# Hybrid attention block on one Trainium2 core: the last two of seven Strassen-like products change places

## The chip, the core and the metric

The kernel runs on one core of one Trainium2 chip as a single program that fills five engines: TensorE (PE, with its weight loads shown apart as PEld), VectorE (DVE), ScalarE (ACT), GpSimd (POOL) and SyncE (SP), of which SP does nothing here but issue DMAs. The metric is device time in microseconds (us) of one execution. The kernel before the change takes 705.33 us in the median of three runs (704.71 to 705.42).

## The reference

The reference computes one decoder block over 512 tokens, with 16 meta tokens put in front (528 positions), at a width of 1024:

```
h    = layer_norm(concat(meta, x))
proj = h @ w_in                      # queries, keys, values, gates of two branches, merge gates
y_d  = rms_norm(softmax(q k^T/8 + alibi) differences @ v)     # 8 heads, two maps each
y_s  = stick_breaking(sigmoid(q k^T/8)) @ v                   # 16 heads of 64
br_d = (y_d * silu(g_d)) @ w_br_diff ;  br_s = (y_s * silu(g_s)) @ w_br_sb
out  = layer_norm(alpha*h + (sigmoid(m_d+b)*br_d + sigmoid(m_s+b)*br_s) @ w_out)[16:]
```

All inputs are float32. The kernel keeps that precision on TensorE by splitting each operand into a high part in the reduced format float32r and a low rest, and adds three products: high by high, high by low, low by high.

## The kernel before, in words

**Units.** The attention is cut into 16 units: eight differential heads, d0 to d7, and eight pairs of stick-breaking heads, s0 to s7. While unit `u` scores, transposes and multiplies its values, the kernel already projects the keys and values of unit `u+1`, the queries of unit `u+2` and some gates. The attention work is a list of steps with due times, the projections are Python generators that yield after each small group of matmuls, and `run` (L574) weaves the two: each yield adds to a clock (0.36 for each row block of the seven products, that is three matmuls), and all steps whose due time has come are emitted there. That gives the program order.

**Who sets the order on the engines.** Between L970 and the late stages the program order is only a priority. A planner, with a cost model of its own, walks through the instructions and gives each engine a fixed order: it puts the next ready instruction by priority, so that work that is later in the program can stand ahead of work that is waiting. On the chip each engine then runs its order as it stands and waits at semaphores. From a point in the last unit (`state["ends"]`, L1039) TensorE's order is the program's, and in the late stages that of all engines is.

**Keys and values by seven products.** For units 4 to 15 (d4 to d7 and s0 to s7) `stage_kv` (L681) makes the 256 columns of keys and values, over 528 positions, with seven block products in place of eight. Each product is 12 matmuls of 128x264 (four row blocks by three parts of the split). They accumulate in three PSUM banks:

- bank x takes products 0, 2, 4 and 6, one on top of the other. Between them x is read: into `u` after 0 (ACT, L711), into the values' buffer `vT` after 2 (ACT, L715), subtracted from `z7` into the second half of `vT` after 4 (DVE, L720), and read as the second half of the keys after 6;
- bank z takes product 1, read into `z7` (ACT, L713), and later product 5, which finishes the first half of `vT` (DVE, L722);
- bank y takes product 3, which with `u` makes the first half of the keys (DVE, L717).

A matmul that adds to a bank has to wait until the reader before it is done. `keys` (L704) splits a finished half of the keys into high and low (ACT L706, DVE L707) in a buffer `ks` (two of them), and `store_k` (L649) sends both halves with eight DMAs on SP's queue (L653, L654) into the tiles `K[0]` and `K[1]`. There is one such pair of tiles for all units, so the stores of unit `u+1` must stand behind the scores of unit `u` in the program.

**Weights.** The seven left factors are four blocks of the weights and sums of them. Two sums come from DMAs that add onto a loaded tile (issued by POOL, L147), and one, which the product into x that comes last needs, is added on DVE (`add`, L170) out of two others. `prep` (L194 to L204 with `hi` at L185 and `lo` at L190) runs four products ahead: it casts a factor to its high part (ACT, L185), takes the rest (DVE, L190), adds the sum if the next factor is one, and fetches further weight tiles (SP, L145) into rings of six and five buffers, as far as those have been used up. The list `items` says which loaded tiles make up each factor, in the order of the products.

**Scores of a stick-breaking pair.** `s_scores` (L900) does one head in five steps, from the longest block of keys down: two matmuls per block (L764), two sigmoids on ACT (L910, L912), a scan and a product on DVE (L916, L917). In unit s0 the sigmoids and the last normalisation of the branch before (L889 to L893, which needs another table of ACT's functions) are chained on ACT in program order (`behind`, L216).

Of the kernel before, what the change touches and what calls it, by code (L numbers as in the profile page):

```python
# [46 lines left out]
def hybrid_block_kernel(ctx: ExitStack, tc: tile.TileContext, x, meta, emb_g, emb_b, w_in, b_gate,  # L47
# [42 lines left out]
    items, names, loads = [], [], []  # L90
    for n, (kind, i) in enumerate(seq):
        if kind in ("BD", "BS", "wd", "ws"):
            if kind[0] == "B":
                tiles = [(w_br_d if kind == "BD" else w_br_s)[:, :, ts(2 * i + m, P)] for m in range(2)]
            else:
                tiles = [w_in[:, :, ds(COL[x + kind[1]] + i * P, P)] for x in "kv"]
            (a11, a12), (a21, a22) = [[w[:, ts(k, 4)] for k in range(2)] for w in tiles]
            ring = "rawa" if kind[0] == "B" else "rawk"
            o = len(loads)
            if ring == "rawa":  # L100
                loads += [(a11, None, "raw"), (a21, (a11,), ring), (a21, (a22,), ring), (a12, None, "raw"), (a22, None, "raw")]
                items += [o, o + 1, (o + 2, o), o + 3, o + 2, o + 4, (None, o + 3)]
            else:
                loads += [(a11, None, "raw"), (a21, (a11,), ring), (a21, (a22, a11), ring), (a12, None, "raw"),
                          (a21, (a22,), ring), (a22, None, "raw")]
                items += [o, o + 1, o + 2, o + 3, o + 4, o + 5, (o + 2, o + 3)]
        elif n < 4:
            items += [None, None]
        else:
            c = COL[kind] + i * P  # L110
            items += [len(loads), len(loads) + 1]
            loads += [(w_in[:, ts(k, 4), c:c + P], None, "raw") for k in range(2)]
        names += [(kind, i)] * (len(items) - len(names))
# [472 lines left out]
    with tc.tile_pool(name="att", bufs=1) as ap:  # L586
# [62 lines left out]
        def store_k():  # L649

            for o, t in staged:
                for c, own, _ in HEADS:
                    nc.sync.dma_start(K[c][LO, :, o].bitcast(F32), t[own].bitcast(F32))  # L653
                    nc.sync.dma_start(K[c][HI, 0, o].bitcast(F32), t[own, 0].bitcast(F32))  # L654
            staged.clear()
# [25 lines left out]
        def stage_kv(unit, kind, n):  # L681

            i = take("w" + kind, n, 7)
            x, z, y = [pj.tile([P, 512], F32, tag="pj", name="q")[:, :H2] for m in range(3)]
            if not kvt:
                kvt.append(pair_of("kvt"))
            u, z7 = kvt[0][:, 0, :H2], kvt[0][:, 0, H2:]

            vT = kvt[0][:, 1, :] if (UNITS.index((kind, n)) - SEVEN) % 2 == 0 else ap.tile([P, L], F32, tag="vT", name="vT")
            of = [(hTh, [hTl[:, k] for k in range(KT)], m, n) for m, n in ((0, 0), (4, 0), (4, 1))]  # L690
            of += [(tS[0], [tL[k % 4][:, k // 4] for k in range(KT)], m, n) for m, n in ((0, 1), (0, 0), (4, 1), (4, 0))]

            def product(q, bank, b, start=True):
                prep(i + q + state["ahead"])
                _, wh, wl = split[i + q]
                bh, bl, m, half = of[b]
                for k in range(4):
                    h, l = bh[:, m + k, ts(half, H2)], bl[m + k][:, ts(half, H2)]
                    for j, (a, b) in enumerate(((wh, h), (wh, l), (wl, h))):
                        pe.matmul(bank, a[:, k, :], b, start=start and k == 0 and j == 0,  # L700
                                  stop=k == 3 and j == 2, skip_group_check=not start)
                    yield 0.36

            def keys(m, src):  # L704
                t = ap.tile([P, 2, H2], F32R, tag="ks", name="ks", bufs=2)
                s.copy(t[:, 0], src)  # L706
                v.tensor_tensor(t[:, 1], src, t[:, 0].bitcast(F32), op=ALU.subtract)  # L707
                staged.append((ts(m, H2), t))

            yield from product(0, x, 0)  # L710
            s.copy(u, x)  # L711
            yield from product(1, z, 5)
            s.copy(z7, z)  # L713
            yield from product(2, x, 4, False)
            s.copy(vT[:, :H2], x)  # L715
            yield from product(3, y, 1)
            v.tensor_tensor(u, y, u, op=ALU.add)  # L717
            keys(0, u)
            yield from product(4, x, 3, False)
            v.tensor_tensor(vT[:, H2:], z7, x, op=ALU.subtract)  # L720
            yield from product(5, z, 6, False)
            v.tensor_tensor(vT[:, :H2], z, vT[:, :H2], op=ALU.subtract)  # L722
            unit["vT"] = vT
            yield from product(6, x, 2, False)
            keys(1, x)
            store_k()

        def values(unit, kind):

# [228 lines left out]
        def spread(gen, t0, dt, count):  # L958
            return [(t0 + dt * m, lambda: next(gen)) for m in range(count)]
# [12 lines left out]
        for u, (kind, n) in enumerate(UNITS):  # L972
            unit = units[u]
# [6 lines left out]
            steps = pending + [(0.6, lambda unit=unit: values(unit, kind))]  # L980
# [9 lines left out]
            if kind == "d":  # L990
                ta = {}
                dt, t0, t1 = TD[u in GATE_AT]
                steps += spread(d_scores(unit, n), 0.0, dt, 10)
                parts = transposed(ta, apads[n % 2])
                steps += [(t0 + 0.7 * m, f) for m, f in enumerate(parts)]
                steps.append((t1, lambda: d_values(unit, ta)))
                pending = [(3.0 if n < 7 else 5.8, lambda unit=unit, n=n: d_norm(unit, n))]
            else:
                if n == 0:
                    diag.append(ap.tile([P, L], F32, tag="bias", name="diag", bufs=2))  # L1000
                    g.memset(diag[0], 0.0)
                    g.tensor_copy(diag[0][:, L - P:], ident)
                    g.memset(v3[:, 1], 0.0)
                    for a in apads:
                        for i in range(NB):
                            g.memset(a[:, ds(AOFF[i] + NKEY[i] - 1, 1)], 0.0)
                if last:
                    ydT = [pair_of("ydT", n=S) for k in range(4)]
                    ydT = [ydT[k % 4][:, k // 4, :] for k in range(8)]
                    ysT = ypool.tile([P, 8, S], F32, tag="ys", name="ysT")  # L1010
                    ysT = [ysT[:, k, :] for k in range(8)]
                    unit["y"] = ysT[7]

                    def fill_in(y, of):
                        placed(lambda: nc.sync.dma_start(y, of), [mybir.EngineType.SP])

                    fill_in(ydT[7], kept["d"][7])
                    for m, (y, of) in enumerate(((ydT, "gd"), (ysT, "gs"))):
                        for j in range(7):
                            steps.append((1.3 + 1.5 * (7 * m + j), lambda o=y[j], x=kept[of][j]: fill_in(o, x)))  # L1020
                    proj += [gate("d", n, lambda: ydT[7]), merge_gate(0, 0), behind_values(merge_gate(0, 1)), merge_gate(0, 2),
                             gate("s", n, lambda: ysT[7])]
                else:
                    if GATE_AT.get(u) == n:
                        yd = gpool.tile([P, S], F32, tag="sg", name="yd")
                        nc.sync.dma_start(yd, kept["d"][n])
                        proj.append(gate("d", n, lambda yd=yd: yd, kept["gd"][n]))
                    else:
                        steps += zip((12.0, 24.0), late_gate(ap, *(kept[x][n] for x in ("d", "r", "gd"))))
                    proj.append(gate("s", n, lambda unit=unit: unit["y"], kept["gs"][n]))  # L1030
                for c in range(2):
                    ta = {}
                    steps += spread(s_scores(unit, c, n == 0), (2.0 + 4.3 * c) if n == 0 else 4.4 * c, 0.85, 5)
                    parts = transposed(ta, apads[c])
                    times = LAST[c] if last else [7.0 + 6.5 * c + 0.7 * m for m in range(3)] + [10.5 + 6.5 * c]
                    steps += zip(times, parts)
                    steps.append((times[3], lambda c=c, ta=ta: s_values(unit, c, n, ta)))
                if last:
                    steps.append((LAST[0][0] - 0.1, lambda: state.update(ends=len(nc.cur_bb.bb.instructions))))  # L1039
# [118 lines left out]
    for p in range(4):  # L1158
        steps = []
# [132 lines left out]
```

## Time and profile before

| | |
|---|---|
| median of three runs | 705.33 us (704.71 to 705.42) |
| the profiled execution | 705.11 us |
| span of its instructions | 703.3 us |
| PE busy | 695.7 us (99%) |
| DVE busy | 570.2 us (81%) |
| ACT busy | 441.5 us (63%) |
| POOL busy | 131.1 us (19%) |
| granted TensorE clock, mean | 0.999 |

The profile comes from one execution. Busy time is the time in which at least one instruction of an engine was running. The profile models when a matmul ends, and matmuls overlap in the pipeline: a 128x264 matmul has a duration of some 0.28 us, while the next one starts 0.12 us after it. So what TensorE really does is read from starts, and from the idle time and the waits that the profile lists. L12 means line 12 of the kernel.

### The profile page before, as it was taken

Reading aid. Unit: us, or ns where it says so; the run is one execution under the profiler, and the core shown is the slowest. Engines: PE = TensorE matmul, PEld = TensorE weight load, DVE = VectorE, ACT = ScalarE, POOL = GpSimd, SP = SyncE. Lnnn points to the kernel's source line nnn. Section 1 sums busy time; section 2 is a strip of 40 time slices with the busy share of each in tenths; the row PEclk is TensorE's granted clock in tenths of the full one; section 3 lists DMA queues with packets and bytes.
Section 4 is the critical chain, followed back from the end, with each engine's and each line's share of the span. In section 5 each row is a group of like instructions: output and inputs, shape, how many; then the busy total and the mean of one; then the engine's idle time right before and its main releaser. Section 6 shows DMA issues by size and latency. Waiting matters only on the chain.

```text
span 703.3 us, 13295 instructions
## 1 busy us (share of the span) xinstructions
PE 695.7 (99%) x4482; PEld 634.8 (90%) x4482; DVE 570.2 (81%) x1226; ACT 441.5 (63%) x1074; POOL 131.1 (19%) x141
## 2 busy tenths in 40 slices
PE   8999999999999999999999999999999999999997
PEld 8999999989899898999989899988888998999885
DVE  6887998978786777989887898977665888688887
ACT  5776767757576687777757687766555456555400
POOL 2243112222222201212121220000011201230012
PEclk9999999999999999999999999999999999999999
DMA  9399547978888786899798977547476749796702
GB/s 290 102 189 188 147 113 177 213 174 188 219 189 184 191 190 181 177 221 207 204 195 216 206 151 198 159 128 240 134 167 132 160 119 232 154 178 184 254 34 120
DMA packets 184214, 124.93 MB, mean 178 GB/s; under 512 B 8993, under 2 KB 168130, under 8 KB 184146
## 3 DMA queue, kind: packets, MB, share of 16 engines
q1 hardware_dynamic: 148050, 102.84, 50.5%
q0 software_dynamic: 35776, 20.19, 23.0%
q10 hardware_dynamic: 320, 1.06, 0.4%
q8 instruction: 35, 0.57, 0.3%
q14 instruction: 33, 0.27, 0.1%
HBM read 93.54 MB, written 9.44 MB: 146 GB/s over the span
## 4 chain that ended last, share of the span: by engine, by line
PE 93%; DVE 2%; ACT 2%; SPq 1%; DMA 1%; issue 0%; POOL 0%; POOLq 0%; ACTq 0%; DVEq 0%
PE q L700 18%; PE ps L500 12%; PE ps L499 12%; PE ps L501 12%; PE q L1083 11%; PE ps L515 6%; PE sc L764 6%; PE pso L1215 5%; PE t L776 4%; PE tv L733 1%; PE av L931 1%; PE av L932 1%; DMA xt<-in_x_dram 1%; PE av L925 1%; PE av L933 1%; PE av L926 1%
## 5 line engine op out<-in xcount | busy, mean ns | idle before, releaser
L500 PE MATMUL ps<-hTl,w 128*128 128x512 f32 x368 | 144.8, 393 | 0.0
L190 DVE TENSOR_TENSOR w<-raw,w 128x512 fp32r<-128x512 f32 x168 | 114.3, 688 | 37.5 <-ACT w L185 35.9
L499 PE MATMUL ps<-hTh,w 128*128 128x512 f32 x368 | 144.6, 393 | 0.0
L501 PE MATMUL ps<-hTh,w 128*128 128x512 f32 x368 | 144.6, 393 | 0.0
L185 ACT CAST w<-raw 128x512 fp32r<-128x512 f32 x168 | 103.4, 627 | 11.6 <-PE ps L501 5.4
L147 POOL DMA_DIRECT2D rawk<-in_w_in_dram x48 | 66.1, 1629 | 116.6 <-DMA rawk<-in_w_in_dram 58.2
L700 PE MATMUL q<-tS,w 128*128 128x264 f32 x384 | 82.6, 289 | 0.0
L1083 PE MATMUL q<-gh,w 128*128 128x256 f32 x448 | 81.4, 283 | 0.2 <-ACT t L1092 0.2
L501 PEld LDWEIGHTS ps<-hTh,w 128*128 128x128 f32 x368 | 69.2, 188 | 13.5
L499 PEld LDWEIGHTS ps<-hTh,w 128*128 128x128 f32 x368 | 69.2, 188 | 13.1
L500 PEld LDWEIGHTS ps<-hTl,w 128*128 128x128 f32 x368 | 69.2, 188 | 13.0
L1083 PEld LDWEIGHTS q<-gh,w 128*128 128x128 f32 x448 | 70.1, 192 | 0.5 <-ACT t L1092 0.4
L764 PE MATMUL sc<-k,A 128*128 128x264 f32 (+3 forms) x320 | 66.0, 299 | 0.0
L700 PEld LDWEIGHTS q<-tS,w 128*128 128x128 f32 x384 | 63.6, 188 | 0.3
L1083 PE MATMUL q<-gl,w 128*128 128x256 f32 x224 | 63.4, 283 | 0.0
L700 PE MATMUL q<-hTh,w 128*128 128x264 f32 x288 | 60.8, 286 | 0.0
L916 DVE TENSOR_TENSOR_SCAN e<-e,diag 128x528 f32<-128x528 f32 (+1 forms) x64 | 54.2, 850 | 5.7 <-ACT e L910 5.7
L700 PE MATMUL q<-tl,w 128*128 128x264 f32 x192 | 54.9, 286 | 0.0
L764 PEld LDWEIGHTS sc<-k,A 128*128 128x128 f32 x320 | 50.1, 189 | 2.3 <-POOL k L607 0.2
L515 PE MATMUL ps<-hTh,w 128*128 128x264 f32 x256 | 51.5, 289 | 0.2 <-ACT k L642 0.2
L700 PEld LDWEIGHTS q<-hTh,w 128*128 128x128 f32 x288 | 47.8, 189 | 1.0 <-DVE vT L720 0.2
L781 ACT CAST ah<-t 128x384 fp32r<-128x384 f32 (+2 forms) x72 | 34.4, 477 | 22.0 <-PE t L776 21.9
(292 smaller groups left out, 1575.9 us busy)
## 6 DMA issues: line engine op xcount, KB each, us to landing
raw<-in_w_in_dram SPq DMA_DIRECT2D x142, 256.0 KB, 3.4
rawk<-in_w_in_dram POOLq DMA_DIRECT2D x48, 256.0 KB, 5.8
rawk<-in_w_in_dram SPq DMA_DIRECT2D x36, 256.0 KB, 4.1
k<-ks SPq DMA_DIRECT2D x60, 132.0 KB, 3.0
raw<-in_w_out_dram SPq DMA_DIRECT2D x16, 256.0 KB, 4.1
k<-ks SPq DMA_DIRECT2D x60, 66.0 KB, 2.8
A<-low SPq DMA_DIRECT2D x28, 128.0 KB, 2.8
raw<-in_w_br_diff_dram SPq DMA_DIRECT2D x12, 256.0 KB, 2.9
```

The lines of the kernel that those rows point to most:

```text
L147: second[l] = [lambda raw=raw, x=x: g.dma_start(raw, x, accum_op=ALU.add) for x in more]
L185: s.copy(wh, raw)
L190: eng.tensor_tensor(wl, raw, wh.bitcast(F32), op=ALU.subtract)
L499: pe.matmul(ps, wh[:, k % 4, :], hTh[:, k, M:], start=(k == 0), stop=False)
L500: pe.matmul(ps, wh[:, k % 4, :], hTl[:, k, M:], start=False, stop=False)
L501: pe.matmul(ps, wl[:, k % 4, :], hTh[:, k, M:], start=False, stop=(k == KT - 1))
L515: pe.matmul(ps[:, :H2], a[:, k % 4, :], b[:, k, ts(c, H2)], start=(k == 0 and m == 0), stop=(k == KT - 1 and m == 2))
L700: pe.matmul(bank, a[:, k, :], b, start=start and k == 0 and j == 0, stop=k == 3 and j == 2, skip_group_check=not start)
L764: pe.matmul(ps[:, :n], q, K[:, m, k0:k0 + n], start=(m == 0), stop=(m == 1))
L916: v.tensor_tensor_scan(rev, rev, diag[0][:, L - nk:][:, ::-1], 0.0, ALU.mult, ALU.max)
L1083: pe.matmul(bank, a[:, k, :], b[:, n, k, :], start=start and k == 0 and m == 0, stop=k == 3 and m == 2, skip_group_check=not start)
L1215: pe.matmul(ps, MH[k][:, ts(t, P)] if m == "h" else ML[:, k, ts(t, P)], WO[c]["hl".index(w)][:, k, r], start=(n == 0), stop=(n == 3 * KT - 1))
```

## The change

The last two of the seven products change places: what was product 6 (into x, finishing the second half of the keys) becomes product 5, and what was product 5 (into z, finishing the first half of the values) becomes product 6. The list of factors changes places with them, so the factor that is a sum is now prepared as the sixth and the plain block as the seventh. The split of the second half of the keys and the eight stores stand ahead of the last product now. As the stores stand 12 matmuls earlier in the program, the second head of unit s0 gets earlier due times (5.2 to 8.6 in place of 6.3 to 9.7), so that its scores still stand ahead of the stores. No instruction is added or removed.

```diff
             else:
                 loads += [(a11, None, "raw"), (a21, (a11,), ring), (a21, (a22, a11), ring), (a12, None, "raw"),
                           (a21, (a22,), ring), (a22, None, "raw")]
-                items += [o, o + 1, o + 2, o + 3, o + 4, o + 5, (o + 2, o + 3)]
+                items += [o, o + 1, o + 2, o + 3, o + 4, (o + 2, o + 3), o + 5]
...
             yield from product(4, x, 3, False)
             v.tensor_tensor(vT[:, H2:], z7, x, op=ALU.subtract)
-            yield from product(5, z, 6, False)
+            yield from product(5, x, 2, False)
+            keys(1, x)
+            store_k()
+            yield from product(6, z, 6, False)
             v.tensor_tensor(vT[:, :H2], z, vT[:, :H2], op=ALU.subtract)
             unit["vT"] = vT
-            yield from product(6, x, 2, False)
-            keys(1, x)
-            store_k()
...
-                    steps += spread(s_scores(unit, c, n == 0), (2.0 + 4.3 * c) if n == 0 else 4.4 * c, 0.85, 5)
+                    steps += spread(s_scores(unit, c, n == 0), (2.0 + 3.2 * c) if n == 0 else 4.4 * c, 0.85, 5)
```

## The prediction

> **What bounds the kernel now.** I read the page first, then the busy time by stretches, then TensorE's waits, and last two of the twelve units in order of time. The page's first part and the stretches (per engine: busy us and number of instructions; the second stretch runs from the first of the seven products to the end of the last):
>
> ```profile
> PE 695.7 (99%) x4482; PEld 634.8 (90%) x4482; DVE 570.2 (81%) x1226; ACT 441.5 (63%) x1074; POOL 131.1 (19%) x141
> ```
>
> ```profile
> 0.00:107.40 107.40, 104.58 (x749) 99.38 (x750) 88.87 (x246) 71.25 (x185) 28.14 (x44) 1.00 0.71 171
> 107.40:452.00 344.60, 344.60 (x2275) 317.27 (x2275) 287.72 (x640) 249.54 (x647) 69.50 (x66) 1.00 0.84 192
> 452.00:650.00 198.00, 197.81 (x1222) 178.04 (x1221) 148.88 (x279) 111.15 (x227) 27.65 (x24) 1.00 0.69 168
> 650.00:703.30 53.30, 48.71 (x242) 40.14 (x240) 44.76 (x63) 9.55 (x17) 5.84 (x7) 0.98 0.37 137
> ```
>
> TensorE is busy for 344.60 of the 344.60 us in which the change acts, at full granted clock (1.00), and for 197.81 of the 198.00 us behind it. Its 7.6 us of idle time lie in the head (2.82) and the tail (4.59), which the change doesn't touch. The waits of matmuls, all five rows, and the one wait of a weight load on a reader of the seven products (total us, times, longest):
>
> ```profile
> PE warm L309 <- POOL ident masks.py:199: 1.4, 1, 1.4
> PE bank L344 <- DVE xn L340: 1.1, 1, 1.1
> PE centred L1237 <- ACT turned L1236: 0.9, 1, 0.9
> PE ps L515 <- ACT k L642: 0.2, 1, 0.2
> PE q L1083 <- ACT t L1092: 0.2, 1, 0.2
> ```
>
> ```profile
> PEld q L700 <- DVE vT L720: 0.2, 1, 0.2
> ```
>
> No row says that a matmul of the seven products, or a score, waits for keys. In twelve units the reader of x cost one weight load 0.2 us, once.
>
> Busy time can hide a short wait, since a 128x264 matmul is shown for 0.28 us and the next starts 0.12 us later. So I look at starts, in the last of the twelve (keys of s7). TensorE, then DVE:
>
> ```profile
> 444.32 0.28 PE L700 MATMUL q<-tl,w 128*128 128x264 f32 x1
> 444.44 0.29 PE L700 MATMUL q<-tS,w 128*128 128x264 f32 x1
> 444.57 0.40 PE L499 MATMUL ps<-hTh,w 128*128 128x512 f32 x1
> ...
> 449.38 0.39 PE L500 MATMUL ps<-hTl,w 128*128 128x512 f32 x1
> 449.61 0.39 PE L501 MATMUL ps<-hTh,w 128*128 128x512 f32 x1
> 449.84 0.29 PE L700 MATMUL q<-hTh,w 128*128 128x264 f32 x1
> ```
>
> ```profile
> 444.42 0.43 DVE L722 TENSOR_TENSOR vT<-q,vT 128x264 f32<-128x264 f32 x1
> ...
> 445.58 0.42 DVE L720 TENSOR_TENSOR vT<-kvt,q 128x264 f32<-128x264 f32 x1
> ```
>
> L722 reads z and L720 reads x after product 4, and L722 comes first: the planner had already put the z product ahead of product 4, though it stands behind it in the program. After x's product 4 ends (last start 444.44), TensorE takes a gate and attention work, and the last x product (on hTh) starts at 449.84, 3.84 us after L720 ended at 446.00. It follows its neighbour at 0.23 us, the step between two 128x512 matmuls (449.38 to 449.61): no wait is hidden there. A tighter hand-over, in the unit at 187 to 215 us (TensorE, then DVE):
>
> ```profile
> 199.06 0.41 PE L700 MATMUL q<-tS,w 128*128 128x264 f32 x2
> 199.31 0.59 PE L764 MATMUL sc<-k,A 128*128 128x272 f32 x4
> 199.73 0.44 PE L885 MATMUL ms<-sqh,onesm 128*128 128x512 f32 x1
> 200.01 0.40 PE L886 MATMUL ms<-sql,onesm 128*128 128x512 f32 x1
> 200.24 0.30 PE L700 MATMUL q<-hTh,w 128*128 128x264 f32 x1
> ```
>
> ```profile
> 199.67 0.42 DVE L720 TENSOR_TENSOR vT<-kvt,q 128x264 f32<-128x264 f32 x1
> ...
> 200.09 0.41 DVE L722 TENSOR_TENSOR vT<-q,vT 128x264 f32<-128x264 f32 x1
> ```
>
> L720 ends at 200.09, the x product starts at 200.24, again 0.23 us behind its neighbour. The planner filled the gap exactly.
>
> [...]
>
> **The change part by part.**
>
> *The matmuls.* 12 units by 84 matmuls, before as after, into the same banks: 0. On TensorE only what is exposed between them can change.
>
> *The new neighbour.* In the program the two x products now stand next to each other, with only L720 between them. From the start of product 4's last matmul to the end of L720 it took 446.00 - 444.44 = 1.56 us in the one unit and 200.09 - 199.06 = 1.03 us in the other; less the usual step of 0.12 us that is 0.9 to 1.4 us which something must cover. The cover is the z product, 12 by 0.12 = 1.4 us, which has been ready since z was copied early on, or the gates and scores that cover it in the rows above. If no cover were left it would be 12 x 0.9 to 12 x 1.4 = 11 to 17 us; at the size of the one wait listed, 12 x 0.2 = 2.4 us. From below: a hidden wait in the old hand-over is at most 0.28 - 0.12 = 0.16 us, 12 x 0.16 = 1.9 us that could be won. I take 0, since both hand-overs shown have nothing hidden and the chain of dependences in x and in z is the same as before; only priorities change.
>
> [...]
>
> *The factors.* Casts, rests and the DVE sum are as many as before; the sum moves one product forward, the plain block one back, and its ring buffer comes free one product later (1.4 us of matmuls), the buffer of the other summand one sooner. What the users of the factors waited for within the stretch (first rest for cast, then cast for TensorE):
>
> ```profile
>   ACT w L185: 16.9, 16
>   PE ps L501: 12.5, 16
>   PE q L700: 4.0, 8
> ```
>
> The casts wait for TensorE to give a buffer back, never for a weight load, so loads land before they are wanted and I take 0. The bound above: eight stores now stand ahead of the last product's load on SP. Here are the second half's first and last issues, the split ahead of them (ACT, DVE), the first score that uses them and the values' transposes:
>
> ```profile
> 452.94 0.52 SPq L654 DMA_DIRECT2D k<-ks  x1
> ...
> 456.76 0.60 SPq L654 DMA_DIRECT2D k<-ks  x1
> ```
>
> ```profile
> 452.23 0.38 ACT L706 CAST ks<-q 128x264 fp32r<-128x264 f32 x1
> ```
>
> ```profile
> 454.19 0.42 DVE L707 TENSOR_TENSOR ks<-q,ks 128x264 fp32r<-128x264 f32 x1
> ```
>
> ```profile
> 461.88 0.65 PE L764 MATMUL sc<-k,A 128*128 128x264 f32 x4
> ...
> 475.72 0.60 PE L733 MATMUL tv<-ident,vT 128*128 128x128 f32 x4
> ```
>
> Eight issues at 0.52 to 0.60 us are 4 to 5 us in which a weight load could stand in line, per unit; bounds 0 and 12 x 5 = 60 us if nothing were prepared ahead.
>
> *Keys sooner, values later.* The split costs 0.38 + 0.42 us, off TensorE, as before. What the swap can win for the keys is at most the 3.84 us by which the x product trailed L720. That would pull the first scores of s7 ahead from 461.88, but TensorE has no gap to fill until then: worth 0. The values get ready one product later, some 1.4 us; their transposes start at 475.72, 30.9 us after L722 ended at 444.85: 0. With the cover gone it would be those 1.4 us once per unit, 17 us.
>
> *Unit s0.* ACT's rows: the table load in front of the last normalisation, and the second head's first sigmoid after it; TensorE's row: the second head's first scores.
>
> ```profile
> 255.12 1.28 ACT L889 ACT_TABLE_LOAD   x1
> ...
> 265.08 0.39 ACT L910 ACTIVATE e<-sc 128x264 f32<-128x264 f32 x1
> ```
>
> ```profile
> 254.44 0.41 PE L764 MATMUL sc<-k,A 128*128 128x264 f32 x2
> ```
>
> The first pair of sigmoids (2 x 0.39 us) now comes ahead of that table load; the rest of the second head stays behind it, and the loads stay as many. A score's bank comes free some 10 us sooner; TensorE has no idle time here either, so 0, with at most 0.8 us of ACT as a loss.
>
> *Sum.* 703.3 us span + 0 + 0 + 0 + 0, and 1.8 us around it: 705.1 us against the profiled 705.11. That execution lies 0.2 us under the median and within the runs' spread; I predict **705.2 us**.
>
> **The rivals.**
>
> *It doesn't do what it says.* The planner goes by readiness: z's product was ahead of x's product 4 already, so the order on TensorE may hardly change and the keys end when they did. For it: L722 ahead of L720 in the one unit. Against it: in the other L722 came after. Time: 705.2 too.
>
> *Faster.* The hand-overs of x hide 0.16 us each after all, and the new order gives it back: 705.2 - 1.9 = 703.3 us. Against it: nothing hidden in either unit shown. More than that TensorE can't give.
>
> *Slower: x behind x.* Place: the first matmul of the new product 5, waiting for L720 with nothing between. It decides once the planner has used up z's product before product 4, as it did for s7, and finds no gate or score ready. Price: 705.2 + 2.4 = 707.6 us at the one wait listed, 716 to 722 us uncovered. For it: L722's early place. Against it: gates and scores filled the same gap in both units.
>
> *Slower: weights late.* SP's queue gets the stores first and a cast waits for its load. One wait as long as an issue, 0.6 us, in each unit: 705.2 + 7 = 712 us. Against it: casts never waited for a load.
>
> **How the numbers follow.** The forecast has 0.52, no change of order 0.23, faster 0.09, x behind x 0.12, late weights 0.04. A measurement tells about 0.2%, 1.4 us, from no change: the first two cases lie within it, so same 0.75, faster 0.09, slower 0.16. The range reaches from 704.2, the forecast less half of the 1.9 us, to 707.6, the cheap form of x behind x; that leaves out some 0.17.
>
> **What would show it right or wrong.** Right: TensorE without idle time up to the tail, L720 with other matmuls between it and x's next product, K's last issue before 456.76. Wrong: a wait of L700 on L720 in many units, casts that wait for a DMA of raw weights, idle TensorE between 107 and 452 us, or a tail that isn't 4.6 us.

## The result and the profile after

The changed kernel takes 710.97 us in the median (709.05 to 711.48), the kernel before on the same chip 705.38 us (704.66 to 705.57). The ratio is 1.0075, with an interval of 1.0064 to 1.0086: the change costs 5.6 us. The profiled execution took 711.42 us with a span of 709.6 us, so 6.3 us are to be found in the traces (709.6 - 703.3).

The page's first part, and the stretches with the bounds used before, without the head; the last one ends with the span:

```profile
PE 699.7 (99%) x4482; PEld 637.1 (90%) x4482; DVE 571.8 (81%) x1226; ACT 441.1 (62%) x1074; POOL 130.1 (18%) x141
```

```profile
107.40:452.00 344.60, 341.94 (x2240) 314.00 (x2239) 284.57 (x632) 244.57 (x635) 67.97 (x65) 1.00 0.84 189
...
650.00:709.60 59.60, 54.82 (x291) 46.07 (x289) 50.49 (x73) 14.27 (x28) 5.83 (x7) 1.00 0.41 143
```

The work is the same (4482 matmuls), but TensorE is now idle for 2.66 us in the stretch of the seven products, where it had no idle time, and gets 2240 matmuls done there in place of 2275. Its waits (total us, times, longest) name the places; rows that stood in the list before are left out:

```profile
PE sc L764 <- DMA k<-ks: 1.8, 1, 1.8
...
PE sc L764 <- ACT e L910: 0.8, 1, 0.8
PE av L925 <- ACT ys L942: 0.4, 1, 0.4
PE ps L499 <- DVE sg L529: 0.3, 1, 0.3
...
PE t L776 <- DVE al L782: 0.2, 1, 0.2
```

No matmul of the seven products waits, and none waits for L720. What waits are scores, twice, and three matmuls of the last unit. First the largest wait, on TensorE at the start of unit s3:

```profile
337.96 0.60 PE L776 MATMUL t<-ident,apad 128*128 128x128 f32 x4
340.37 0.48 PE L764 MATMUL sc<-k,A 128*128 128x264 f32 x2 [1.81 <-DMA k<-ks]
...
341.58 0.42 PE L700 MATMUL q<-tl,w 128*128 128x264 f32 x1
341.80 0.65 PE L700 MATMUL q<-tS,w 128*128 128x264 f32 x2
```

The scores on the second half of the keys come 1.98 us after their turn, worked out from the starts as everywhere below (340.37, less the start of the last transpose in front at 338.28, less its usual step of 0.11). Behind the gap a second loss follows: from 341.58 to 341.80 a step of 128x264 takes 0.22 us and not 0.12. Thirteen steps in a row are stretched like that, 1.37 us in all. The stretches show why (the granted clock is the third number from the right):

```profile
340.30:341.20 0.90, 0.83 (x7) 0.86 (x8) 0.00 (x0) 0.32 (x2) 0.00 (x0) 0.99 1.17 318
341.20:344.30 3.10, 3.10 (x17) 3.10 (x15) 2.57 (x3) 1.41 (x5) 0.00 (x0) 0.50 0.44 112
```

The trace has the clock at 0.50 from 341.18 to 344.59: TensorE runs for 3.4 us at half clock. PE counts as busy all the while (3.10 of 3.10 us in the second row), so the busy share doesn't show it.

The second wait of scores is that at the start of unit s5, 1.01 us at 406.1; the list names ACT L910 for it, but by the trace that was long done, and the store of K landed at 407.12, 0.14 us ahead of the score. The third place is the last unit. TensorE there, after and, for comparison, before:

```profile
474.19 0.71 PE L764 MATMUL sc<-k,A 128*128 128x144 f32 x4
475.27 0.49 PE L925 MATMUL av<-ah,V 128*128 128x512 f32 x1 [0.38 <-ACT ys L942]
475.92 0.55 PE L776 MATMUL t<-ident,apad 128*128 128x128 f32 x3 [0.15 <-DVE al L782]
476.72 0.50 PE L499 MATMUL ps<-hTh,w 128*128 128x512 f32 x1 [0.25 <-DVE sg L529]
```

```profile
467.08 0.86 PE L764 MATMUL sc<-k,A 128*128 128x400 f32 x4
467.78 0.39 PE L501 MATMUL ps<-hTh,w 128*128 128x512 f32 x1
...
469.16 0.40 PE L501 MATMUL ps<-hTh,w 128*128 128x512 f32 x1
469.40 0.49 PE L776 MATMUL t<-ident,apad 128*128 128x128 f32 x3
469.64 0.48 PE L925 MATMUL av<-ah,V 128*128 128x512 f32 x1
```

Before, seven gate matmuls (467.78 to 469.16) lay between the scores and the next product with the values; ACT copied the bank out in their shadow (L942, 467.53 to 468.11). After, they have been used up earlier, and the product follows the scores and waits for ACT: 0.54, 0.42 and 0.41 us, 1.37 in all.

The sum: 1.98 + 1.37 + 1.01 + 1.37 = 5.7 us of the 6.3. The rest is in steps that are each under 0.2 us too long.

**Why the keys of s3 are late.** They are finished later than before, not sooner. The rows of their last steps, before: DVE (the reader of x), TensorE (the last product into x, first and last rows), ACT and DVE (the split), SP (the store that the scores wait for, its landing, and the queries' DMAs), and the scores.

```profile
320.50 0.43 DVE L720 TENSOR_TENSOR vT<-kvt,q 128x264 f32<-128x264 f32 x1
...
328.93 0.41 DVE L707 TENSOR_TENSOR ks<-q,ks 128x264 fp32r<-128x264 f32 x1
```

```profile
324.54 0.29 PE L700 MATMUL q<-hTh,w 128*128 128x264 f32 x1
...
337.42 0.65 PE L764 MATMUL sc<-k,A 128*128 128x264 f32 x4
```

```profile
330.04 0.88 SPq L653 DMA_DIRECT2D k<-ks  x1
...
335.25 3.21 SPq L624 DMA_DIRECT2D A<-low  x2
```

```profile
DMA to landing us min/median/max: 4.6/4.6/4.6
```

And after:

```profile
323.73 0.42 DVE L720 TENSOR_TENSOR vT<-kvt,q 128x264 f32<-128x264 f32 x1
...
334.12 0.43 DVE L707 TENSOR_TENSOR ks<-q,ks 128x264 fp32r<-128x264 f32 x1
```

```profile
328.72 0.37 PE L700 MATMUL q<-hTh,w 128*128 128x264 f32 x1
```

```profile
335.06 1.37 SPq L624 DMA_DIRECT2D A<-low  x2
336.53 1.28 SPq L653 DMA_DIRECT2D k<-ks  x2
```

The rows of SP don't show which of the two heads a store is for; the built program does. The first scores of s3 are the first head's, and they need the second half of `K[0]`: before, that store is the one at 330.04 (the stores after it, up to 333.32, fill `K[1]` for the second head), and after, it is the first of the two at 336.53.

L720 ends 3.2 us later than before (324.15 for 320.93), the last product into x starts 4.2 us later, behind gate and query matmuls, the split on DVE is 5.2 us later, and on SP the store now stands behind two of the queries' DMAs: 336.53 for 330.04, 6.5 us later. Before, it landed 4.65 us after its issue, at 334.69, and the scores on this half started at 337.67 (the third of the four in the row at 337.42), so 3.0 us were to spare. After, it lands 3.7 us after its issue, at 340.23. That is 5.5 us later than before, while the turn of the scores comes only 0.7 us later (338.39): 5.5 - 3.0 - 0.7 = 1.8 us are missing, and the scores start 0.14 us after the landing. The slack was not small; the store was moved by more than it, and the prediction didn't work out how far the new order would move it. In each of the seven executions with a wait at s3, here and below, the score starts 0.09 to 0.14 us after this store has landed.

### The profile page after: what moved, and what is told of

Read it like the earlier page. It is cut to its first block, busy times and chain, and to the rows that moved or that the text cites. A ratio compares the mean times of both kernels' runs of the same rounds, so it can differ in the third digit from the quotient of the medians.

```text
span 709.6 us, 13282 instructions
## 1 busy us (share of the span) xinstructions
PE 699.7 (99%) x4482; PEld 637.1 (90%) x4482; DVE 571.8 (81%) x1226; ACT 441.1 (62%) x1074; POOL 130.1 (18%) x141
## 4 chain that ended last, share of the span: by engine, by line
PE 80%; issue 7%; DMA 4%; DVE 3%; ACT 2%; SPq 2%; POOL 1%; POOLq 0%; DVEq 0%; ACTq 0%
PE q L700 14%; PE q L1083 11%; PE ps L499 10%; PE ps L500 10%; PE ps L501 10%; PE ps L515 6%; PE pso L1215 5%; PE sc L764 5%; PE t L776 3%; DMA rawk<-in_w_in_dram 3%; DMA raw<-in_w_in_dram 1%; PE tv L733 1%; DVE w L190 1%; PE av L931 1%; POOL rawk L147 1%
## 5 line engine op out<-in xcount | busy, mean ns | idle before, releaser
L501 PE MATMUL ps<-hTh,w 128*128 128x512 f32 x368 | 144.5, 393 | 0.0
L147 POOL DMA_DIRECT2D rawk<-in_w_in_dram x48 | 64.1, 1582 | 145.8 <-DMA rawk<-in_w_in_dram 77.4
L700 PE MATMUL q<-tS,w 128*128 128x264 f32 x384 | 82.9, 292 | 0.0
L501 PEld LDWEIGHTS ps<-hTh,w 128*128 128x128 f32 x368 | 69.2, 188 | 13.4
L700 PEld LDWEIGHTS q<-tS,w 128*128 128x128 f32 x384 | 64.1, 191 | 0.7 <-ACT gr L541 0.2
L700 PE MATMUL q<-hTh,w 128*128 128x264 f32 x288 | 62.1, 288 | 0.0
L700 PE MATMUL q<-tl,w 128*128 128x264 f32 x192 | 55.1, 287 | 0.0
L700 PEld LDWEIGHTS q<-hTh,w 128*128 128x128 f32 x288 | 48.1, 189 | 1.0 <-DVE vT L720 0.2
L190 DVE TENSOR_TENSOR w<-rawk,w 128x512 fp32r<-128x512 f32 x48 | 32.7, 685 | 14.6 <-ACT w L185 14.6
```

The costliest lines, as they stand in the source:

```text
L147: second[l] = [lambda raw=raw, x=x: g.dma_start(raw, x, accum_op=ALU.add) for x in more]
L190: eng.tensor_tensor(wl, raw, wh.bitcast(F32), op=ALU.subtract)
L501: pe.matmul(ps, wl[:, k % 4, :], hTh[:, k, M:], start=False, stop=(k == KT - 1))
```

## The experiments

The edit has three separable parts: the due times of unit s0's second head, the order of the two products, and the order in which the factors are prepared. The first four runs take them apart, the next three take away one suspected cause each from the changed kernel (whose repetition runs beside them), and the last three put the cures together and try one unit alone. "Wait" below is always the excess of a step on TensorE over its usual length.

**The due times alone.** The kernel before with this line:

```diff
-                    steps += spread(s_scores(unit, c, n == 0), (2.0 + 4.3 * c) if n == 0 else 4.4 * c, 0.85, 5)
+                    steps += spread(s_scores(unit, c, n == 0), (2.0 + 3.2 * c) if n == 0 else 4.4 * c, 0.85, 5)
```

> The kernel before with only the earlier due times of unit s0's second head (5.2 to 8.6). Theory A, the products' order is what costs: no change, 705.4 +- 0.7 us. Theory B, unit s0's sigmoids, now ahead of the last normalisation's table load, shift all later units: 709 to 711 us. Theory C, the order of the factors: 705.4 us.

Measured: 706.43 us (706.03 to 707.53) beside 705.10, ratio 1.0016 (1.0007 to 1.0026). That is none of the values expected (705.4 +- 0.7, or 709 to 711). One wait, where the changed kernel has its largest:

```profile
PE sc L764 <- DMA k<-ks: 0.9, 1, 0.9
```

It is 1.08 us by the starts, and the 1.3 us of difference is that wait and little else. A due time in unit s0 is paid in unit s3: the planner puts some 730 matmuls from s0 on at other places. On SP the queries' DMAs stand ahead of K's last stores here too (335.27 and 336.54 us). The keys of s3 are as late here as in the changed kernel: the split on DVE starts at 334.23 (334.12 there), the store into `K[0]` at 336.54 (336.53 there). So the due times make them late.

**The order of the products alone** (the factors in the new order with it, due times as before; so that the scores of s0 still stand ahead of the stores, those of unit s1 stay behind its last product):

```diff
+            yield from product(5, x, 2, False)
+            keys(1, x)
+            if (kind, n) != ("s", 1):
+                store_k()
+            yield from product(6, z, 6, False)
...
+            store_k()
             unit["vT"] = vT
```

> The changed kernel with unit s0's old due times (6.3 to 9.7); so that the scores still stand ahead of the stores, the stores of s1's keys, and of those alone, stand behind the last product. Theory A: the whole loss stays, 709 to 711.5 us, with scores waiting for K's stores at the starts of s3 and s5. Theory B: 705.4 +- 0.7 us. Theory C: 709 to 711.5 us.

Measured: 706.92 us (706.53 to 707.22), ratio 1.0020 (1.0010 to 1.0029). The time lies between the values expected, and there is no wait at s3 or s5, where theory A had them; all of it lies in the last unit: 0.54, 0.43, 0.41 and 0.37 us, 1.75 in all, for a difference of 1.8. The keys of s3 are hardly late here: the split starts at 328.70 (328.93 before the change), the store into `K[0]` at 331.57 (330.04).

**The order of the factors alone.** The kernel before, with the factors prepared in the new order and each product taking its own:

```diff
-                items += [o, o + 1, o + 2, o + 3, o + 4, o + 5, (o + 2, o + 3)]
+                items += [o, o + 1, o + 2, o + 3, o + 4, (o + 2, o + 3), o + 5]
...
-            yield from product(5, z, 6, False)
+            yield from product(5, z, 6, False, 6)
...
-            yield from product(6, x, 2, False)
+            yield from product(6, x, 2, False, 5)
```

> The kernel before, its products in the old order, but the sum prepared as the sixth factor and the plain block as the seventh. TensorE's order comes out as before. Theory A and B: 705.4 +- 0.7 us. Theory C, the plain block's factor is late and POOL's adding DMAs change places: most of the loss, 708 us or more.

Measured: 705.23 us (704.53 to 706.90), ratio 0.9999 (0.9990 to 1.0009). No wait. By itself this part is free, as predicted. SP and POOL at s3 (for the runs further down):

```profile
329.96 1.72 SPq L653 DMA_DIRECT2D k<-ks  x1
```

```profile
334.16 1.27 POOL L147 DMA_DIRECT2D rawk<-in_w_in_dram  x1 [5.94 <-DMA rawk<-in_w_in_dram]
```

The store into `K[0]` that the first scores need goes out at 329.96, 4.2 us ahead of POOL's accumulating DMA; the last store, for the second head, goes out at 334.05, just ahead of it, and lands after 2.4 us.

**The changed kernel with the factors in the old order**, the same edit the other way round:

> The changed kernel, its products in the new order, but the factors prepared in the old order. TensorE's order comes out as in the changed kernel. Theory A and B: 709 to 711.5 us as the changed kernel. Theory C: near 705.4 us.

Measured: 707.54 us (706.98 to 708.58), ratio 1.0028 (1.0017 to 1.0040). The wait at s3 is 0.71 us, that at s5 0.42, those of the last unit 1.38: 2.5 us for a difference of 2.4. That is neither of the two values expected. Due times and products together cost 2.4 us, less than the sum of each alone (1.3 + 1.8), and the factors, free by themselves, cost 3.2 us on top of them (5.6 - 2.4, each less its own kernel before), although TensorE's order in this run is that of the changed kernel. So their price is not in TensorE's order but in what feeds it.

**The changed kernel again**, as the base of the next three:

> The changed kernel as it stands, as the base of the three runs beside it. Theory A (the loss is the sum of a few waits of TensorE: 1.98 us for the keys of unit s3 and 1.4 us at half pitch behind it, 1.0 us for the keys of unit s5, 1.4 us for copies in the last unit): 710.5 to 711.5 us with the same waits at the same places. Theory B (the loss is a general slowing by contention and the waits are only where it shows): the time may be the same, but the waits stand at other places in another profile.

Measured: 710.94 us (710.17 to 711.46) beside 705.33, ratio 1.0076 (1.0059 to 1.0093). The waits: 2.87 us at s3 (1.98 in the first profile) with 1.29 us at half clock behind it, none at s5 (1.01 in the first), 1.38 in the last unit. The places are the same, and so is the sum of the two waits for keys (2.9 and 3.0 us), but how it is shared between s3 and s5 differs from one execution to the next.

**POOL's second accumulating DMA later.** What the factors' order changes on POOL is seen at s3. Before and after:

```profile
324.26 4.26 POOL L147 DMA_DIRECT2D rawk<-in_w_in_dram  x3
...
343.36 1.66 POOL L147 DMA_DIRECT2D rawk<-in_w_in_dram  x1
```

```profile
323.36 4.23 POOL L147 DMA_DIRECT2D rawk<-in_w_in_dram  x3
333.14 1.27 POOL L147 DMA_DIRECT2D rawk<-in_w_in_dram  x1 [5.55 <-DMA rawk<-in_w_in_dram]
```

The fourth accumulating DMA goes out at 333.1 us, just ahead of K's stores, and not at 343.4. One number puts it back; the orders of TensorE, ACT, DVE and SP stay those of the changed kernel:

```diff
-                            later.append((state["n"] + 3 + 3 * n, lambda l=l: added(l)))
+                            later.append((state["n"] + 3 + 4 * n, lambda l=l: added(l)))
```

> The changed kernel with one number of the prefetch list altered, so that POOL's second accumulating DMA of a sum stands one step later, about where it stands before the change; the orders of TensorE, ScalarE, VectorE and SyncE are those of the changed kernel. Theory A with POOL's early accumulating DMA as the cause of what the order of factors adds (its transfer lies across the stores of K: landing 3.7 us after issue, 2.9 where it doesn't): the wait of s3 falls from 2.0 to 1.1 us or less, the half pitch behind it goes, 707.5 to 709 us. Rival A2 (the factors add to it through the orders of ScalarE, VectorE and SyncE): unchanged, 711 us.

Measured: 707.60 us (707.14 to 707.78), ratio 1.0030 (1.0018 to 1.0042). The stores of K's second half, and who waited:

```profile
L653 SPq DMA_DIRECT2D k<-ks x2: 616/616/617, 336.5 to 337.2; - x2
...
  PE sc L764: 0.6, 1
...
DMA to landing us min/median/max: 2.4/2.4/2.4
```

Issued at the same time as in the changed kernel (336.5 us), they land after 2.4 us where it took 3.7 there and 4.3 in its repetition. The wait falls to 0.77 us, the half clock is gone, and with it 3.3 of the 5.6 us. That is about the 3.2 us of the factors. With the factors alone POOL's DMA is as early (334.16 us), but there the stores are out ahead of it; only when the due times have made K late do the two meet.

**K's stores ahead of the queries' DMAs.** The changed kernel, with an order on SP for units s3 and later:

```diff
                 nc.sync.dma_start(o.bitcast(F32), src.bitcast(F32))
+                for c in range(2 if kind == "s" and n >= 3 else 0):
+                    follow(nc.cur_bb.bb.instructions[-1], state["kst", c])
...
                     nc.sync.dma_start(K[c][LO, :, o].bitcast(F32), t[own].bitcast(F32))
+                    state["kst", c] = nc.cur_bb.bb.instructions[-1]
```

> The changed kernel with an order on SyncE alone: in the units from s3 on the three DMAs that move the queries' halves stand behind the DMAs that store the second half of K, not ahead of them; 13 places of SyncE differ, all at s3, and no other engine's order does. Theory A (the first scores of s3 wait for these stores): they are issued at 334.3 to 335.2 us instead of 336.5, land at 337.2 to 338.8 ahead of the scores at 338.4, the wait of 2.0 us falls to 0 to 0.4 and the 13 matmuls at 220 ns go back to 121: 707.3 to 708 us. Theory B: the wait stands elsewhere, 711 us.

Measured: 708.25 us (707.73 to 708.68), ratio 1.0041 (1.0026 to 1.0056). The time is 0.25 us over the range expected. The wait at s3 is 0.80 us, more than the 0 to 0.4 expected, and the half clock is gone. SP's rows and the landing show what was missed:

```profile
335.50 1.53 SPq L655 DMA_DIRECT2D k<-ks  x2
337.08 0.60 SPq L624 DMA_DIRECT2D A<-A  x1
```

```profile
DMA to landing us min/median/max: 4.5/4.5/4.5
```

The stores go out 1.0 us sooner, but with POOL's DMA still ahead of them (333.8 us) they take 4.5 us, for 2.4 in the run before this one. The two causes are separate: place in SP's queue, and what is under way beside the transfer.

**Unit s5's products in the old order**, the rest of the changed kernel as it is:

```diff
+            last = UNITS.index((kind, n)) in (13,)
+            if last:
+                yield from product(5, z, 6, False, 6)
+                v.tensor_tensor(vT[:, :H2], z, vT[:, :H2], op=ALU.subtract)
+            yield from product(6 if last else 5, x, 2, False, 5)
             keys(1, x)
             store_k()
+            if not last:
+                yield from product(6, z, 6, False)
```

> The changed kernel with the last two products of unit s5 alone in the old order, the factors prepared as in the changed kernel. TensorE's order is then that of the run with the due times alone (matmuls behind the 2605th stand as before the change). Theory A: the wait for the keys of s5 (1.0 us) and the three of the last unit (1.4 us) are gone, those of s3 stay (1.1 to 2.0 us, with 0 or 1.4 us behind them): 706.4 to 708.6 us. Rival: the waits of the last unit come from its own two products, or from all units together: 709.5 us or more.

Measured: 710.07 us (708.55 to 713.92), ratio 1.0081 (1.0050 to 1.0111), above the range of theory A and with a wide spread, and the execution profiled, 713.6 us, is one of its longest:

```profile
PE sc L769 <- DMA k<-ks: 3.9, 2, 2.5
PE bank L344 <- DVE xn L340: 1.9, 1, 1.9
```

The three waits of the last unit are gone, as expected (another one, of 0.86 us, stands further on). The wait at s5 is not: 1.53 us, beside 2.65 at s3 with 1.19 at half clock behind it. So the last unit's waits come from the exchange in s5, and the wait at s5 does not; that half of the expectation was wrong. At s5 the store into `K[0]` took 4.6 us to land (405.45 to 410.04), and the score started at 410.17. 1.7 us of this execution were lost in the head, where the kernels are the same: a wait of 1.9 us (the second row, 1.1 before the change), and behind it, too, a stretch at half clock.

**Both small edits together** (POOL's DMA later and K's stores first):

> The changed kernel with both small edits: the stores of K's second half ahead of the queries' DMAs on SyncE from unit s3 on, and POOL's second accumulating DMA one step later. Theory A: each alone left a wait of 0.8 us at s3 (stores issued at 335.5 us and landing 4 us later, or issued at 336.5 and landing 2.4 us later); together they are issued at 335.5 and land at 337.9 to 338.4, about when the scores are due: 0 to 0.3 us is left there, the three waits of the last unit (1.4 us) stay: 706.5 to 707.1 us. Rival: the 0.8 us left in each is another cause (ScalarE's or VectorE's order, the products being late), not helped by either: 707.4 us or more.

Measured: 707.09 us (706.86 to 707.77) beside 705.25, ratio 1.0025 (1.0015 to 1.0036). At s3 the stores land 3.0 to 3.1 us after their issue. SP and TensorE there:

```profile
334.66 1.36 SPq L655 DMA_DIRECT2D k<-ks  x2
```

```profile
338.04 0.60 PE L779 MATMUL t<-ident,apad 128*128 128x128 f32 x4
338.40 0.49 PE L767 MATMUL sc<-k,A 128*128 128x264 f32 x2
```

The scores follow the transposes without a gap. Only the last unit's three waits are left (1.38 us, for a difference of 1.8).

**The same with unit s5 in the old order:**

> The same two edits, and the last two products of unit s5 in the old order. Theory A (the whole loss is these waits): no wait of TensorE over 0.3 us is left in the units, and the time is that of the kernel before, 705.0 to 705.9 us, although 700 matmuls stand at other places than before the change. Theory B (something beside the waits costs time): 706.5 us or more.

Measured: 706.08 us (705.73 to 707.27), ratio 1.0012 (1.0003 to 1.0021). That is 0.2 us over the range expected. Two waits are left, 0.23 us at s5 and one of 0.64 us in the last unit (0.5 of them listed):

```profile
PE av L934 <- ACT af L820: 0.5, 1, 0.5
```

Their sum, 0.87, is near the difference of 0.8 us of the medians; the execution profiled is a long one, 2.0 us over the kernel before, and 0.5 us of that lie behind TensorE's last matmul. The row was there in two other kernels (0.86 and 0.37 us above), so it isn't of these edits. Some 730 matmuls stand at other places than before the change, and cost nothing beside the waits.

**Unit s5 alone.** The kernel before, with the exchange in this one unit (and the factors in the new order, which costs nothing):

```diff
+            last = UNITS.index((kind, n)) in (4, 5, 6, 7, 8, 9, 10, 11, 12, 14, 15)
```

> The kernel before with the last two products exchanged in unit s5 alone (and the factors prepared in the changed kernel's order, which by itself cost nothing); due times as before. TensorE's order is that of before up to its 2546th matmul and from its 3107th on. Theory A (the waits of the last unit come from the exchange in s5, which frees the gate's matmuls to go ahead, so that they no longer lie between the last unit's scores and its products with the values): three waits of 0.54, 0.43 and 0.41 us at 470 to 473 us, no other, 706.4 to 706.9 us. Rival (the last unit's waits come from the exchange in all units, or in the last): 705.2 us.

Measured: 706.66 us (706.05 to 708.05), ratio 1.0021 (1.0012 to 1.0031). In the last unit:

```profile
471.14 0.49 PE L930 MATMUL av<-ah,V 128*128 128x512 f32 x1 [0.38 <-ACT ys L947]
471.79 0.55 PE L781 MATMUL t<-ident,apad 128*128 128x128 f32 x3 [0.15 <-DVE al L787]
472.58 0.50 PE L499 MATMUL ps<-hTh,w 128*128 128x512 f32 x1 [0.25 <-DVE sg L529]
```

These are the three rows of the changed kernel, from an exchange two units earlier. Not expected were short waits beside them (0.50 us at s2, 0.20 at s5, 0.19 further on). The exchange in s5 alone makes 1.4 of the 5.6 us.

All of them side by side, each time less the kernel before of the same chip, and the waits of the profiled execution (us):

| kernel | time less before | s3 | half clock behind it | s5 | last unit | sum |
|---|---|---|---|---|---|---|
| changed, first profile | 5.6 (6.0 profiled) | 1.98 | 1.37 | 1.01 | 1.37 | 5.7 |
| changed, again | 5.6 (6.1 profiled) | 2.87 | 1.29 | 0 | 1.38 | 5.5 |
| due times alone | 1.3 | 1.08 | 0 | 0 | 0 | 1.1 |
| products alone | 1.8 | 0 | 0 | 0 | 1.75 | 1.8 |
| factors alone | 0.1 | 0 | 0 | 0 | 0 | 0 |
| factors undone | 2.4 (2.8 profiled) | 0.71 | 0 | 0.42 | 1.38 | 2.5 |
| POOL's DMA later | 2.3 | 0.77 | 0 | 0 | 1.38 | 2.2 |
| K's stores first | 2.9 (3.2 profiled) | 0.80 | 0 | 0 | 1.37 | 2.2 |
| s5 in the old order | 4.7 (8.3 profiled) | 2.65 | 1.19 | 1.53 | 0.86 | 6.2 |
| stores and POOL | 1.8 | 0 | 0 | 0 | 1.38 | 1.4 |
| these and s5 | 0.8 (2.0 profiled) | 0 | 0 | 0.23 | 0.64 | 0.9 |
| s5 alone | 1.4 (2.3 profiled) | 0 | 0 | 0.20 | 1.57 | 2.3 with 0.50 at s2 |

Of the loss of the execution profiled, the waits account to within 0.6 us in nine of the twelve; they fall short by 1.0 us with K's stores first, by 1.1 in the run with all three edits, and by 2.1 with s5 in the old order, where 1.7 lie in the head. No kernel is faster than the one before beyond the noise.

## Why the prediction was wrong

It said 705.2 us, with 704.2 to 707.6; the kernel takes 711.0.

- **The bound** was read rightly: in that stretch TensorE had no idle time and could only lose. The step that is missing is how near it was to losing. The prediction looked at one hand-over of keys, that of s7, and paired the wrong rows: the last issue (456.76) is a store for the second head. The first head's last store went out at 455.43, and its scores on that half started at 462.12, 6.7 us later. In s3 the same two are 7.6 us apart (330.04 and 337.67), in s5 only 4.0 (398.57 and 402.55). So s3, where the largest wait came, was not the tightest: what counts is also how far the new order moves the store, 6.5 us there.
- **The matmuls** (0) and **the new neighbour** (0): right as far as they went. (The row at 199.06 holds two matmuls, the second at 199.18, so the 1.03 us are 0.9; nothing hangs on it.) No L700 waits for L720, and the rival *x behind x* didn't come. But their price was looked for at the exchanged products only. The run with s5 alone shows that the exchange costs 1.4 us two units later, because it lets gate matmuls be used up that the last unit needed as cover.
- **Keys sooner, values later** (0): this step failed. It took for granted that the keys come no later, as product 5 stands in front. In s3 their split came 5.2 us later and the store that the scores wait for 6.5 us. The claim that TensorE has no gap to fill until the scores held, and said nothing about scores that have to wait.
- **Unit s0** (0, at most 0.8 us of ACT): this step failed first, as it is what makes the keys of s3 late. Its effect on ACT is not what counts. The due times reorder TensorE up to s3 and move the hand-over of keys there: 1.3 us alone, with the split and the store as late as in the changed kernel, and the wait of the changed kernel needs them, since with the products alone the keys are hardly late and the wait isn't there.
- **The factors** (0, bound 60 us): right alone (0.1 us), wrong in company: 3.2 us. The term looked at SP and at the casts; those still wait for TensorE almost alone (casts 15.1 us for L501 and 4.2 us for L700), never for a load. That the order of the factors also moves POOL's accumulating DMAs, and these lie across K's stores, was not priced. The rival *weights late* therefore didn't come either: it is the weights that come early and make K late.
- **The tail** is as predicted: 4.78 us idle for 4.59 (59.60 - 54.82).
- **It doesn't do what it says**: half of this rival came true. In the order that the planner laid, the exchange moves no matmul in units d4 to d7, since z's product stood ahead already. But the keys were not left where they were, by the due times above all.

What stays open: why the wait for keys is now all at s3 and now shared with s5. At s5 the store into `K[0]` took 5.1 us to land in the first profile, where the score waited 1.01 us for it, and 2.7 in the repetition, where none did; what made the difference isn't known. At s3, K's last stores take 3.7, 4.3, 4.5 and 4.3 to 4.7 us to land in the four executions in which they go out late and POOL's accumulating DMA has been issued 1.7 to 3.4 us ahead of them, and 2.4 to 3.1 us in the five in which they go out late without it; in the run with POOL's DMA later, POOL's order alone was altered. By what they get into each other's way was not tried. Nor is it the only case of a slow landing: before the change the store at 330.04 took 4.65 us, with three of POOL's accumulating DMAs issued 4.3 to 5.8 us ahead of it.

## What to carry to other kernels

Where an engine has no idle time, a reordering has little to win and much to lose. Its price is found at the hand-overs whose order it moves: work out, for each of the units and not for one, how far the new order moves the last transfer, and set that against the slack between its landing and its reader. Here a slack of 3.0 us was overrun by a landing 5.5 us later. With a planner, an edit is priced by the orders that it lays on every engine, and those differ far from the edited lines (here three and two units away, on TensorE, SP and POOL), so a term "only priorities change" is no 0. And a part that is free by itself may not be free beside the others: the factors cost 0.1 us alone and 3.2 us on top of the rest.

## What the runs showed of the hardware

In three of the profiles a wait of scores has a second price. With each of the three waits of 1.98, 2.65 and 2.87 us come 3.4 us at a granted clock of 0.50: 12 or 13 stretched steps in a row (0.22 us for 0.12 between two 128x264 matmuls), 1.2 to 1.4 us in all. The wait of 1.9 us in the head of the run with s5 in the old order has such a stretch, too. Both of that run:

```profile
7.94:11.36 3.42, 3.42 (x17) 3.42 (x18) 2.73 (x7) 2.52 (x8) 0.74 (x2) 0.50 1.07 357
342.45:345.86 3.41, 3.04 (x14) 3.07 (x15) 1.69 (x2) 1.46 (x4) 0.00 (x0) 0.50 0.70 170
```

Behind the waits of scores of 0.71 to 1.53 us nothing follows. The granted clock is 1.00 from 330 to 350 us in the four runs that wait 0.71, 0.77, 0.80 and 1.08 us at s3, and 1.00 from 344.59 us to the end in the first profile, which waits 1.01 us at s5. The stretch behind the longest of them, of 1.53 us (s5 in the old order):

```profile
410.00:414.00 4.00, 3.83 (x29) 3.79 (x30) 2.91 (x5) 2.75 (x7) 0.00 (x0) 1.00 0.68 214
```

So in these runs the second loss of 1.2 to 1.4 us came with waits of 1.9 us and more and not with those of 0.71 to 1.53 us, and bringing the wait at s3 under that saved 3.3 us where the waits themselves shrank by some 2. The moment of the switch doesn't follow from the gap alone: it comes 0.8 and 0.9 us after TensorE starts again in the two profiles of the changed kernel, but 0.4 us before it with s5 in the old order (342.45 and 342.82). In the first profile the trace's record of the clock starts at 6.67 us with 1.00, and the clock is halved at 341.18 and full again at 344.59, 334.51 and 337.92 us later: 98 and 99 times 3.4133 us, the length of the half-clock stretch (3.413 us). Before the change the record starts at 4.98 us, and the clock is halved at 701.30 in the tail, 696.32 us later: 204 times that length. With s5 in the old order the two stretches above start 334.51 us apart, 98 times again. Whether it matters where a gap lies between two such moments, beside its length, is open: no run here separates the two.
